# A hybrid decoder trunk on one core: the last two FFN pairs with tokens on partitions, attention scores in strict turn through one pipeline, two FFN pairs ahead, and activation parts side by side

## The chip, the cores and the metric

The kernel runs on one core of one Trainium2 chip. Times are device microseconds (us) of one execution; with one core, that core's time is the time of the kernel. Engines are named as in the profile: PE (TensorE), DVE (VectorE), ACT (ScalarE), POOL (GpSimd), SP (SyncE, here only an issuer of DMAs).

## The reference

`x` is (1, 512, 1024) float32, so 512 tokens of 1024 channels. The trunk has two layers and a final norm; D_FF is 2816.

```python
for l in range(2):
    if l == 0:
        h = h + conformer_conv(rmsnorm(h, norm_mix[0]), ...)   # pw1 + GLU, causal depthwise conv of 31, LayerNorm, silu, pw2
    else:
        if l == 1:
            k, v = split(rmsnorm(h, norm_kv) @ w_kv)           # 4 KV heads of 64
        q = (rmsnorm(h, norm_mix[1]) @ w_q)                    # 16 heads of 64
        h = h + banded_sink_attention(q, k, v, sinks, rel_bias) @ w_o
    gate, up = split(rmsnorm(h, norm_ffn[l]) @ w_up)
    h = h + (silu(gate) * up) @ w_down
return rmsnorm(h, norm_final)
```

The attention is banded: each block of 128 queries sees its own block of keys and the one before, with a relative-position bias, a window of 128 and one learned sink per head in the softmax.

## The kernel before, in words

**Layout.** Activations lie transposed: channels on partitions, the 512 tokens on the free axis. The residual `h` is one SBUF tile of [128, 8, 512] float32 that stays for the whole kernel; `x` comes in transposed and the result goes out transposed (`outT`).

**Products.** From the first FFN on, each fp32 product is made of three fp32r matmuls (`mm3`, L258 to L264): weights high part by activations high part, weights high by activations low, weights low by activations high, the first two at L262 and L263 and the third at L264, all into one PSUM bank (a bank holds 128 x 512 float32; there are eight). Weights are the stationary operand, activations (256 or 512 tokens wide) the moving one.

**Weights.** They stream from HBM in chunks of 512 KB in the order of `PLAN` (`chunk_plan`, L51 to L92). `get` (L244) hands out the next chunk, and `advance` (L191) issues the DMA six chunks ahead and the split three chunks ahead: ACT casts the high part (`whi`, L203), DVE subtracts to get the low part (`wlo`, L204). There are four buffers of each. The order of instructions on each engine is fixed by a scheduler when the kernel is built; `tc.issue_after` ties one instruction behind another.

**Layer 0.** Conv and the first part of the FFN (pairs 0 to 4 of 11; a pair is 256 hidden channels) are done for one half of the tokens (256) and then the other. While PE is at the first half's FFN, the depthwise conv of the second half runs beside it on POOL, ACT and DVE as background jobs (L207 to L226; taps L596 to L615), paced by due points. `ffn_part` (L423) calls `ffn_up` (L451), then two groups of down products; up takes four chunks for each pair: two halves of the 1024 input channels by gate and up. The normed input `xg` (`x0`) is an `Act` (L266): high tile and low tile apart. It is filled by `Next.on_h` (L511), which for each of the eight channel tiles has ACT scale (L382) and DVE subtract (L383), while `Rms` (L327) squares, adds (L340) and later makes the inverse root. `evac` (L455) takes a finished pair out of PSUM. The second part of FFN 0 (pairs 5 to 10) runs on all 512 tokens.

**Attention.** K and V, then q in two groups of eight heads (`down_group` with keys "q"), each ended by `q_evac` (L905). The heads are done in 16 units (`unit`, L912), each four heads of one group and one block of 128 queries: 12 score matmuls (L928) on 64 of the 128 rows, which go by turns to the two row halves (g = 0 and 1), four bias-and-minimum operations on DVE (L931), four exponentials on ACT (L938), a reciprocal (L940), four scalings on POOL (L942), transposes by PE (L950), cast and subtraction (L953, L954), the products with V by `mm3`, and cast and subtraction of the output (L968, L969). `pipeline(gp)` (L972) staggers the eight units of a group: one step starts a unit and advances three others. Pipeline `p0` (group 0) steps between the matmuls of q's second group, and what is left is drained behind it (L996); `p1` steps between the matmuls of the output projection's first half (o part 0) and is drained behind it (L1011).

**Layer 1's FFN and the end.** Pairs 0 to 5 and 6 to 8 run on all tokens. The last two pairs (`LAST`, 9 and 10) are followed by class `Fin` (L1020): two halves of 256 tokens, channels on partitions; each fetches the four down chunks, so they are fetched twice. `rows` adds to `h` (L1047), squares (L1051), and sums over channels by adds on POOL and matmuls with a column of ones (L1039); `sums` makes the mean (L1070), the inverse root by pow on POOL (L1072) and a diagonal (L1074); `spread` (L1084, L1088) brings the inverse root to all partitions by a matmul; `out_pool` (L1100) and `out_dve` (L1106) scale and store (L1096), two channel tiles by POOL and six by DVE.

## Time and profile before

| what | value |
|---|---|
| time of three runs | 1115.78, 1117.93, 1115.91 us (median 1115.91) |
| the profiled execution | 1115.77 us |
| its span in the profile | 1114.0 us, 15803 instructions |
| busy: PE, DVE, ACT, POOL | 1098.9, 662.3, 502.6, 322.1 us |
| mean granted TensorE clock | 0.993 of full speed |
| moved by DMA | 125.00 MB, 112 GB/s on average |

The span runs from the first to the last recorded instruction; the time of an execution holds a little more. A group line reads: line, engine, operation, out<-in, shapes, how often, then busy us and mean ns of one, then the idle time of that engine just before those instructions and what ended it. In a table of windows each engine has its busy us and instruction count, then the granted clock, the share of the DMA engines and GB/s. In a timeline, a row is start, duration, engine, line; a wait stands in brackets with what ended it. In the chain of waits each piece is the time that the last-ending chain spent there.

### The profile page before, as it was taken

To read this page: it belongs to the slowest core of one execution; us is meant where nothing else is said; L and a number is where in the kernel's file an instruction comes from. 1 tells how busy PE (TensorE), PEld (TensorE's weight loads), DVE (VectorE), ACT (ScalarE), POOL (GpSimd) and SP (SyncE) were. 2 spreads that over 40 slices of the span, in tenths; PEclk is the share of its full clock that TensorE was granted. 3 is DMA by queue.
4 is the path that set the end of the run, shared out by engine and by line. 5 is a ranking of instruction groups with operands and counts; after the bars stand their busy time and mean duration, and the time that the engine had idled before them with its cause. 6 is when DMAs were issued, how large, how long until landed. Compare 5 with 4: busy or idle time off the path is not lost.

```text
span 1114.0 us, 15803 instructions
## 1 busy us (share of the span) xinstructions
PE 1098.9 (99%) x5994; PEld 955.7 (86%) x5994; DVE 662.3 (59%) x1074; ACT 502.6 (45%) x891; POOL 322.1 (29%) x420
## 2 busy tenths in 40 slices
PE   9999998999999999999999999999999999999997
PEld 8888898999999888888888788888888888888886
DVE  4999999977665454443575686683444333444455
ACT  4786787765543232232343574553322211332233
POOL 4999699700100021110230332241111100110014
PEclk9999998999999999999999999999999999999998
DMA  9227044576655423332322201023233333323332
GB/s 362 100 31 84 25 168 136 183 247 190 189 174 184 135 95 101 105 97 95 95 95 87 75 29 48 30 95 95 95 95 95 97 102 103 96 95 95 95 95 77
DMA packets 40857, 125.00 MB, mean 112 GB/s; under 512 B 4395, under 2 KB 12748, under 8 KB 40780
## 3 DMA queue, kind: packets, MB, share of 16 engines
q1 hardware_dynamic: 40204, 123.55, 36.2%
q8 instruction: 47, 0.77, 0.3%
q10 hardware_dynamic: 576, 0.44, 0.1%
q14 instruction: 30, 0.25, 0.1%
HBM read 118.73 MB, written 5.24 MB: 111 GB/s over the span
## 4 chain that ended last, share of the span: by engine, by line
PE 90%; DVE 5%; ACT 2%; issue 1%; POOL 1%; DMA 0%; SPq 0%; POOLq 0%; DVEq 0%; ACTq 0%
PE bank L263 26%; PE bank L262 26%; PE bank L264 26%; PE bank L562 8%; PE bank L928 1%; DVE quad L383 1%; PE bank L649 1%; ACT pr L603 1%; DVE bank L611 1%; PE bank L950 1%; DVE wlo L204 1%; DMA h<-in_xT_dram 0%; DVE sc L931 0%; PE bank L375 0%; DVE ptl L954 0%
## 5 line engine op out<-in xcount | busy, mean ns | idle before, releaser
L263 PE MATMUL bank<-quad,whi 128*128 128x512 f32 (+1 forms) x1536 | 535.2, 349 | 3.8 <-DVE quad L383 3.7
L262 PE MATMUL bank<-quad,whi 128*128 128x512 f32 (+1 forms) x1536 | 534.8, 350 | 0.5 <-ACT quad L968 0.5
L264 PE MATMUL bank<-quad,wlo 128*128 128x512 f32 (+1 forms) x1536 | 535.1, 348 | 0.0
L204 DVE TENSOR_TENSOR wlo<-raw,whi 128x1024 fp32r<-128x1024 f32 x194 | 262.5, 1354 | 322.4 <-ACT whi L203 312.3
L203 ACT CAST whi<-raw 128x1024 fp32r<-128x1024 f32 x194 | 203.3, 1049 | 360.0 <-PE bank L263 319.3
L263 PEld LDWEIGHTS bank<-quad,whi 128*128 128x128 f32 x1536 | 292.0, 190 | 40.9 <-DVE quad L383 5.0
L262 PEld LDWEIGHTS bank<-quad,whi 128*128 128x128 f32 x1536 | 291.7, 190 | 38.5 <-ACT quad L968 0.9
L264 PEld LDWEIGHTS bank<-quad,wlo 128*128 128x128 f32 x1536 | 292.1, 190 | 36.8 <-issue 0.2
L472 POOL TENSOR_TENSOR tmp<-tmp,tmp 128x512 f32<-128x512 f32 x34 | 48.4, 1425 | 486.7 <-DVE tmp L471 473.1
L604 POOL TENSOR_TENSOR pr<-pr,pr 128x256 f32<-128x256 f32 x208 | 161.6, 825 | 11.0 <-ACT pr L603 11.0
L611 DVE SCALAR_TENSOR_TENSOR bank<-apad,wdw,bank 128x256 f32<-128x256 f32 x248 | 113.2, 485 | 3.6
L562 PE MATMUL bank<-quad,w 128*128 128x256 f32 x512 | 114.2, 382 | 0.6 <-DMA w<-in_W_dram 0.5
L562 PEld LDWEIGHTS bank<-quad,w 128*128 128x128 f32 x512 | 97.4, 191 | 15.4 <-DVE quad L537 1.7
L603 ACT ACTIVATE pr<-apad,wdw 128x256 f32<-128x256 f32 x208 | 99.0, 503 | 20.8 <-POOL pr L604 18.1
L340 POOL TENSOR_TENSOR tmp<-tmp,tmp 128x256 f32<-128x256 f32 (+1 forms) x35 | 38.8, 1109 | 138.6 <-ACT tmp L336 109.1
L470 ACT ACTIVATE tmp<-tmp 128x512 f32<-128x512 f32 x34 | 21.4, 632 | 92.9 <-DVE tmp L469 92.9
L942 POOL TENSOR_SCALAR sc<-sc,sm 128x256 f32<-128x256 f32 (+1 forms) x64 | 30.0, 489 | 79.4 <-DVE sm L940 79.4
L386 ACT CAST quad<-tmp 128x512 fp32r<-128x512 f32 (+1 forms) x50 | 29.1, 586 | 30.4 <-POOL tmp L472 26.6
L471 DVE TENSOR_TENSOR tmp<-bank,rsbc 128x512 f32<-128x512 f32 x34 | 23.5, 691 | 32.4 <-PE bank L264 32.4
L383 DVE SCALAR_TENSOR_TENSOR quad<-h,prm,quad 128x512 fp32r<-128x512 f32 (+1 forms) x40 | 39.5, 1020 | 0.5 <-ACT quad L382 0.4
L938 ACT ACTIVATE sc<-sc,m 128x257 f32<-128x257 f32 (+1 forms) x64 | 30.3, 476 | 15.4 <-DVE m L931 13.7
L387 DVE TENSOR_TENSOR quad<-tmp,quad 128x512 fp32r<-128x512 f32 (+1 forms) x50 | 32.8, 661 | 2.5 <-ACT quad L386 2.5
(140 smaller groups left out, 747.0 us busy)
## 6 DMA issues: line engine op xcount, KB each, us to landing
raw<-in_W_dram SPq DMA_DIRECT2D x202, 512.0 KB, 3.5
w<-in_W_dram SPq DMA_DIRECT2D x15, 512.0 KB, 9.7
fd<-fs SPq DMA_DIRECT2D x1, 3072.0 KB, 33.8
h<-in_xT_dram SPq DMA_DIRECT2D x8, 256.0 KB, 5.9
bias<-fd SPq DMA_DIRECT2D x8, 256.0 KB, 5.5
out_dram<-res SPq DMA_DIRECT2D x14, 128.0 KB, 1.8
w<-in_W_dram SPq DMA_DIRECT2D x2, 256.0 KB, 4.1
out_dram<-res ACTq DMA_DIRECT2D x2, 128.0 KB, 2.7
```

Of the source, the lines that this page charges most:

```text
L203: nc.scalar.copy(hi, r)
L204: lo_engine[0].tensor_sub(lo, r, f32(hi))
L262: nc.tensor.matmul(out, w[0], x[0], start=start, stop=False)
L263: nc.tensor.matmul(out, w[0], x[1], start=False, stop=False)
L264: nc.tensor.matmul(out, w[1], x[0], start=False, stop=stop)
L340: self.eng.tensor_add(sq, self.acc, sq)
L383: nc.vector.scalar_tensor_tensor(dst[1], src, g, f32(dst[0]), op0=ALU.mult, op1=ALU.subtract)
L472: nc.gpsimd.tensor_mul(t2, t1, t2)
L562: mm = nc.tensor.matmul(self.pb[:, w * W2:(w + 1) * W2], w1[ct][:, w, k, :], x[k] if x else xg[k][:, tok], start=k == 0, stop=k == KT - 1)
L603: on_act = nc.scalar.mul(pr, a[:, j:j + W2], tap(j))
L604: on_pool = nc.gpsimd.tensor_add(pr, acc, pr)
L611: on_dve = nc.vector.scalar_tensor_tensor(yt if i == nd - 1 else c, src, tap(i), c if i else self.shift, op0=ALU.mult, op1=ALU.add)
```

## The change

- **Two pairs ahead.** `up_order(lo, hi, ahead)` gives the order of the up chunks. In the FFN of the first token half the second half of pair 0 and the first half of pair 1 change places: (0,0), (1,0), (0,1), (1,1), then as before. `PLAN` follows. Both pairs' `evac` stand behind (1,1).
- **Parts side by side.** `x0` becomes `Pairs`: high and low part of a channel tile lie next to each other in one tile ([128, 2, 2, 512]). In the FFN of the second token half (`twin=True`) a product is two matmuls (`mm2`): the weights' high part by both parts at once, 512 wide, into the two halves of a bank, and the weights' low part by the high part, 256 wide, into the first half. Each output tile then takes a whole bank (four a pair); the two halves are added when they are taken out (ACT copy, DVE add), and POOL does the multiplication that DVE did.
- **Attention.** Each unit starts with a 1x1 matmul, and its 12 score matmuls are tied behind each other and behind it by `issue_after`. There is one pipeline over 16 units. It steps between the matmuls of q's second group, whose `q_evac` is done bank by bank as each finishes; four more steps follow; then it steps in o part 0 and is drained behind that.
- **The end.** `Block` takes the place of `Fin`: four blocks of 128 tokens, tokens on partitions. The residual comes into PSUM by eight transposes of `h` tiles into two banks, and the down products of the last two pairs are added to it there with the activations as stationary operand and the weights as moving one (512 wide, three matmuls per 128 channels and half of D). ACT squares a bank with a running sum, DVE and POOL make the inverse root, DVE multiplies by the final gain (fetched once as a row to all partitions), ACT and DVE scale by the inverse root, and the result goes out as (512, 1024). The first two blocks share each fetched down chunk, and the other two use the same splits, so the four chunks are fetched once.

```diff
@@ -48,6 +48,13 @@
 NPARAM = _c
 
 
+def up_order(lo, hi, ahead):
+    o = [(pair, half) for pair in range(lo, hi) for half in range(2)]
+    if ahead:
+        o[1], o[2] = o[2], o[1]
+    return o
+
+
...
+    class Pairs:
+
+        def __init__(self, n, w=512):
+            self.per = 1024 // w
+            self.q = [quads.tile([P, self.per, 2, w], F32R, tag="quad", name=uid("quad")) for _ in range(-(-n // self.per))]
+
+        def both(self, i):
+            return self.q[i // self.per][:, i % self.per]
+
+        def __getitem__(self, i):
+            b = self.both(i)
+            return b[:, 0, :], b[:, 1, :]
+
+    def mm2(out, w, x, start, stop):
+
+        first, second = (w[0], x, out), (w[1], x[:, 0, :], out[:, 0, :])
+        if stop:
+            first, second = second, first
+        nc.tensor.matmul(first[2], first[0], first[1], start=start, stop=False)
+        nc.tensor.matmul(second[2], second[0], second[1], start=False, stop=stop)
 
...
-            if on_step is not None and ci == nk - 1:
+                if on_m is not None and ci == nk - 1 and k == 1:
+                    on_m(m)
+                    if m % 2:
+                        on_step()
+            if on_step is not None and on_m is None and ci == nk - 1:
                 on_step()
                 on_step()
...
+            if twin:
+                banks = [bank().rearrange("p (a s) -> p a s", a=2) for _ in range(4)]
+                for kp in range(lo, hi):
+                    whi, wlo = get("down", layer, kp, g)
+                    order = [(k, m) for k in range(2) for m in range(4)]
+                    if kp == hi - 1:
+                        order = [(k, m) for m in range(4) for k in range(2)]
+                    for k, m in order:
+                        sl = slice(m * P, (m + 1) * P)
+                        mm2(banks[m], (whi[:, k, sl], wlo[:, k, sl]), hid.both(2 * (kp - lo) + k),
+                            kp == lo and k == 0, kp == hi - 1 and k == 1)
+                rs_bc = rms.step2()
+                for m, b in enumerate(banks):
+                    t, hm = temp()[:, 0:w], h[g * 4 + m][:, tok]
+                    nc.scalar.copy(t, b[:, 1, :])
+                    nc.vector.tensor_add(t, b[:, 0, :], t)
+                    nc.gpsimd.tensor_mul(t, t, rs_bc)
+                    nc.vector.tensor_add(hm, hm, t)
+                continue
...
+            if twin:
+                t1, t2 = temp(), temp()
+                for which, t in enumerate((t1, t2)):
+                    for m in range(2):
+                        b = banks[which * 2 + m]
+                        tm = t[:, m * w:(m + 1) * w]
+                        nc.scalar.copy(tm, b[:, 1, :])
+                        nc.vector.tensor_add(tm, b[:, 0, :], tm)
+                t1v, t2v = (t.rearrange("p (a s) -> p a s", a=2) for t in (t1, t2))
+                nc.gpsimd.tensor_mul(t1v, t1v, rs_bc.unsqueeze(1).to_broadcast([P, 2, w]))
+                nc.scalar.activation(t1, t1, AF.Silu)
+                nc.gpsimd.tensor_mul(t2, t1, t2)
+                i = 2 * (pair - lo)
+                q = hid.q[i // 4][:, i % 4:i % 4 + 2]
+                nc.scalar.copy(q[:, :, 0, :], t2v)
+                nc.vector.tensor_sub(q[:, :, 1, :], t2v, f32(q[:, :, 0, :]))
+                return
...
+        opened, pending = {}, []
+        for pair, half in up_order(lo, hi, ahead):
+            if half == 0:
+                if twin:
+                    opened[pair] = [bank().rearrange("p (a s) -> p a s", a=2) for _ in range(4)]
+                    opened[pair] = opened[pair], opened[pair]
+                elif w == 256:
+                    full = [bank(), bank()]
+                    opened[pair] = full, [b[:, e * w:(e + 1) * w] for b in full for e in range(2)]
+                else:
+                    full = accs(w)
+                    opened[pair] = full, full
+            full, banks = opened[pair]
+            for which in range(2):
+                whi, wlo = get("up", layer, pair, half, which)
+                order = [(k, m) for k in range(4) for m in range(2)]
+                if half == 1:
+                    order = [(k, m) for m in range(2) for k in range(4)]
+                for k, m in order:
+                    sl = slice(m * P, (m + 1) * P)
+                    if twin:
+                        mm2(banks[which * 2 + m], (whi[:, k, sl], wlo[:, k, sl]), xg.both(half * 4 + k)[:, :, tok],
+                            half == 0 and k == 0, half == 1 and k == 3)
+                        continue
+                    mm3(banks[which * 2 + m], (whi[:, k, sl], wlo[:, k, sl]), cut(xg[half * 4 + k], tok),
+                        half == 0 and k == 0 and opens(m, w), half == 1 and k == 3 and closes(m, w))
+            if half == 0 and w == 512 or half == 0 and twin:
                 rms.step1()
+            if half == 1 and w == 256 and pair == lo and not twin:
+                rms.step1()
+            if half == 1:
                 pending.append((pair, full))
-            else:
-                evac(pair, full)
+            if half == (1 if ahead else 0) or w == 512 or twin or pair > lo:
+                if not (half == 1 and pair == lo and w == 256 and not twin):
+                    for p in pending:
+                        evac(*p)
+                    pending = []
         return hid
...
-        x0 = {"ffn0": Act(KT)}
+        x0 = {"ffn0": Pairs(KT)}
...
+    ffn_part(0, 0, x0["ffn0"], HALF[1], n1.rms, twin=True)
...
+        def q_evac(g, banks, ms=range(4)):
+            if qs[g] is None:
+                qs[g] = (quad(), quad())
+            for m in ms:
                 t = temp()
                 nc.vector.scalar_tensor_tensor(t, banks[m], -HD ** -0.5, rs_bc, op0=ALU.mult, op1=ALU.mult)
                 split((qs[g][0][:, m, :], qs[g][1][:, m, :]), t)
...
+
+            mm = nc.tensor.matmul(pbs[1][0:1, 0, 0:1], ones_c, ones_c, start=True, stop=True)
             for e in range(2):
                 j = 2 * jp + e
                 for a, b in ((0, 0), (0, 1), (1, 0)):
                     for g in range(2):
-                        nc.tensor.matmul(pbs[g][:, e, :], qs[gp][a][rows[g], j, qt],
-                                         kq[rows[g], b, gp, k0:k0 + BAND], start=a + b == 0, stop=a == 1)
+                        with tc.issue_after(mm.ins):
+                            mm = nc.tensor.matmul(pbs[g][:, e, :], qs[gp][a][rows[g], j, qt],
+                                                  kq[rows[g], b, gp, k0:k0 + BAND], start=a + b == 0, stop=a == 1)
...
-        def pipeline(gp):
-            units = [unit(gp, jp, n) for n in range(NBLK) for jp in range(2)]
-            done = 0
+        def pipeline():
+            units = [unit(gp, jp, n) for gp in range(2) for n in range(NBLK) for jp in range(2)]
             for t in range(len(units) + 4):
                 for d in (4, 3, 1, 0):
...
-        p0 = pipeline(0)
+        pipe = pipeline()
+
+        def step():
+            next(pipe, None)
+
         banks = [bank() for _ in range(4)]
         down_group([(("q", kp, 1), 2 * kp) for kp in range(4)], lambda kt: xq[kt], banks,
-                   on_step=lambda: next(p0, None))
-        q_evac(1, banks)
-        drain(p0)
-        p1 = pipeline(1)
+                   on_step=step, on_m=lambda m: q_evac(1, banks, [m]))
+        for _ in range(4):
+            step()
         nxt = Next(("ffn1",))
...
+                drain(pipe)
...
+
+    res = ctx.enter_context(tc.tile_pool(name="res", bufs=2))
+    gain = res.tile([P, D], F32, tag="gain", name="gain", bufs=1)
+    nc.sync.dma_start(gain, fin.to_broadcast([P, D]))
     hid = ffn_up(1, *LAST, nxt.x["ffn1"], ALL, nxt.rms)
...
+    chunks = {}
+
+    class Block:
+        def __init__(self, b):
+            self.b, self.tok = b, slice(b * P, (b + 1) * P)
+            self.banks = [bank(), bank()]
+            self.ss = small.tile([P, 4], F32, tag="ss", name=uid("ss"))
+            self.hg = []
+            for i in range(KT):
+                c = (i % 4) * P
+                nc.tensor.matmul(self.banks[i // 4][:, c:c + P], h[i][:, self.tok], ident, is_transpose=True,
+                                 start=i % 4 == 0, stop=False)
 
         def down(self, kp, g):
+            if (kp, g) not in chunks:
+                chunks[kp, g] = get("down", 1, kp, g)
+            whi, wlo = chunks[kp, g]
+            for k in range(2):
+                a = cut(hid[2 * (kp - LAST[0]) + k], self.tok)
+                for n, (x, w) in enumerate(((a[0], whi), (a[0], wlo), (a[1], whi))):
+                    nc.tensor.matmul(self.banks[g], x, w[:, k, :], start=False, stop=kp == LAST[1] - 1 and k == 1 and n == 2)
+
+        def half(self, g):
+            ss, b = self.ss, self.banks[g]
+            sq = res.tile([P, 512], F32, tag="sq", name=uid("sq"))
+            nc.scalar.activation(sq, b, AF.Square, accum_out=ss[:, g:g + 1])
+            if g == 0:
+                nc.vector.tensor_scalar(ss[:, 2:3], ss[:, 0:1], 1.0 / D, EPS, op0=ALU.mult, op1=ALU.add)
+            else:
+                nc.vector.scalar_tensor_tensor(ss[:, 3:4], ss[:, 1:2], 1.0 / D, ss[:, 2:3], op0=ALU.mult, op1=ALU.add)
+                rs = small.tile([P, 1], F32, tag="rs1", name=uid("rs1"))
+                nc.gpsimd.tensor_tensor(rs, ss[:, 3:4], mhalf[:, 0:1], op=ALU.pow)
+                self.rs = rs
+            t = res.tile([P, 512], F32, tag="hg", name=uid("hg"), bufs=5)
+            nc.vector.tensor_mul(t, b, gain[:, g * 512:(g + 1) * 512])
+            self.hg.append(t)
+
+        def out(self, w):
+            for c in range(0, 512, w):
+                for g, t in enumerate(self.hg):
+                    t = t[:, c:c + w]
+                    if g:
+                        nc.vector.tensor_scalar(t, t, self.rs[:, 0:1], None, op0=ALU.mult)
+                    else:
+                        nc.scalar.mul(t, t, self.rs[:, 0:1])
+                    (nc.sync if g else nc.scalar).dma_start(out[self.tok, g * 512 + c:g * 512 + c + w], t)
+
+    pairs = range(*LAST)
+    first = [Block(0), Block(1)]
+    for kp in pairs:
+        for g in range(2):
+            for bl in first:
+                bl.down(kp, g)
+                if kp == LAST[1] - 1:
+                    bl.half(g)
+    for bl in first:
+        bl.out(512)
+    for b in range(2, NBLK):
+        bl = Block(b)
+        for g in range(2):
+            for kp in pairs:
+                bl.down(kp, g)
+            bl.half(g)
+        bl.out(512 if b < NBLK - 1 else 256)
```

All of `Fin`, with `fill` and what calls it, is removed; `kernel` passes the final gain as a row and takes the output as (512, 1024).

179 lines of the change are left out of this document (20 added, 159 removed).

## The prediction

> **What bounds the kernel now.** I read the busy shares first, then the chain of work that ended last by engine, the waits of TensorE (PE), and the table of windows.
>
> ```profile
> PE 1098.9 (99%) x5994; PEld 955.7 (86%) x5994; DVE 662.3 (59%) x1074; ACT 502.6 (45%) x891; POOL 322.1 (29%) x420
> ...
> PE 90%; DVE 5%; ACT 2%; issue 1%; POOL 1%; DMA 0%; SPq 0%; POOLq 0%; DVEq 0%; ACTq 0%
> ```
> ```profile
> PE bank L263 <- DVE quad L383: 3.7, 3, 1.9
> ```
> ```profile
> core 0: us, PE busy (x) PEld busy (x) DVE busy (x) ACT busy (x) POOL busy (x), PEclk, DMA share, GB/s
> ...
> 167.00:177.30 10.30, 7.33 (x34) 6.63 (x33) 10.20 (x11) 7.92 (x17) 10.30 (x11) 0.67 0.28 95
> ...
> 250.00:300.00 50.00, 50.00 (x419) 50.00 (x419) 36.37 (x47) 26.38 (x41) 6.48 (x8) 1.00 0.62 187
> ...
> 640.00:660.00 20.00, 19.66 (x140) 17.18 (x139) 19.05 (x55) 16.40 (x49) 9.09 (x20) 1.00 0.14 49
> 760.00:1000.00 240.00, 240.00 (x1059) 198.38 (x1058) 99.09 (x103) 67.92 (x79) 22.76 (x17) 1.00 0.31 97
> ```
>
> PE is the bound, at a full granted clock, almost everywhere: 90% of the chain. So time comes from two sources only: fewer or cheaper matmuls, or one of the few places where PE stands. The largest wait that the trace names is 3.7 us, behind DVE's L383, in the stretch at 167 us; there the clock also falls to 0.67. Two spacings come out of the windows and price all that follows: 50/419 = **0.1193 us** for a 256-wide matmul, 240/1059 = **0.2266 us** for a 512-wide one (a busy time of one matmul is longer, since they are pipelined). A 512-wide matmul is 0.012 cheaper than two of 256. DVE and ACT hold 59% and 45%, so their work is free except where a window shows them full: 167 to 177 and the middle of attention, 640 to 660.
>
> The profiled execution took 1115.77 us, its span 1114.0, so 1.77 lie outside the span. The sum is made against 1115.77, which is 0.14 below the median 1115.91; that difference is nothing here. About 0.2% (2.2 us) is what a measurement of this kernel can tell from no change.
>
> **A: two pairs ahead (first-half FFN of layer 0).** Up's third chunk needs the upper four tiles of xg, which DVE is late with:
>
> ```profile
> 161.06 0.47 PE L262 MATMUL bank<-quad,whi 128*128 128x256 f32 x1
> ...
> 168.16 0.94 DVE L383 SCALAR_TENSOR_TENSOR quad<-h,prm,quad 128x256 fp32r<-128x256 f32 x1
> 169.16 0.39 PE L263 MATMUL bank<-quad,whi 128*128 128x256 f32 x1 [1.88 <-DVE quad L383]
> 170.90 0.58 PE L263 MATMUL bank<-quad,whi 128*128 128x256 f32 x1 [0.99 <-DVE quad L383]
> ...
> 175.13 3.42 DVE L204 TENSOR_TENSOR wlo<-raw,whi 128x1024 fp32r<-128x1024 f32 x2
> ...
> 177.31 0.31 PE L264 MATMUL bank<-quad,wlo 128*128 128x256 f32 x1
> ...
> 179.62 0.36 PE L262 MATMUL bank<-quad,whi 128*128 128x256 f32 x1
> ```
>
> The new order puts pair 1's two first-half chunks ahead of that wait. Four chunks of 24 matmuls run from 161.06 to 161.06 + 96×0.1193 = 172.5 with nothing late. Then the fifth needs xg's upper tiles and its own wlo. That wlo is still made on DVE behind the same eight L383/sum operations: the L204 pair that starts at 175.13 gives it at about 175.13 + 1.71, or 177.3 with one more conv tap ahead of it. So **the wait doesn't vanish, it turns into one of 4.8 us for wlo** (172.5 to 177.3). The fifth chunk starts 2.3 us earlier than the 179.62 of now. Against that: PE's clock fell after waits of 1.88 and 0.99, and after a wait of 4.8 the clock would fall as well, and a third of it missing (0.67) over some 4.5 us costs 1.5; and the next chunks' wlo come one by one from a DVE and a POOL that are full (10.20 and 10.30 of 10.3 us), so the lead is likely eaten there. Bounds: +2.3 saved if the lead is kept, 2 lost if the cold clock and the supply both count. I take **0**.
>
> **B: x's parts side by side (second-half FFN of layer 0).** In that FFN 480 up and 240 down matmuls of 256 become 240 of 512 (whi by [xhi|xlo]) and 240 of 256 (wlo by xhi). Per triple: 3×0.1193 = 0.3579 becomes 0.2266 + 0.1193 = 0.3459, so 240×0.012 = **+2.9**. The added adds and copies (estimates from the rows of like width under C: ACT about 6.9, DVE 7.8, POOL 2.9 us a pair) fit under a pair's 32×0.3459 = 11.07 us of PE, and a pair now holds four banks until then, with eight in all. Bounds 0 (the saved share is lost in bank waits) to 2.9; I take the row's value, since both widths are measured in long undisturbed windows. The Trainium skill, "TensorE: Matmul & The Clock Gate", section "Back-to-back issue gap", gives an isolated gap of N/2.4 + 2.5 ns, so 109 and 216 ns; it also says that this over-counts a sustained stream at large N. By that formula B would be an estimated 0.6. The trace's spacings speak against it (119.3 and 226.6 ns).
>
> **C: attention.** Scores first:
>
> ```profile
> 616.18 0.97 PE L928 MATMUL bank<-kq,quad 64*128 64x256 f32 x12
> 617.08 0.50 PE L262 MATMUL bank<-quad,whi 128*128 128x512 f32 x1
> ...
> 628.29 0.97 PE L928 MATMUL bank<-kq,quad 64*128 64x256 f32 x6
> 629.19 0.49 PE L262 MATMUL bank<-quad,whi 128*128 128x512 f32 x1
> ...
> 646.13 0.40 PE L264 MATMUL bank<-quad,wlo 128*128 128x512 f32 x1
> ...
> 664.13 0.73 PE L262 MATMUL bank<-quad,whi 128*128 128x512 f32 x2 [0.19 <-ACT quad L968]
> ```
> ```profile
> 646.65 0.87 PE bank L950 x8
> ...
> 653.83 0.91 PE bank L928 x6
> 654.73 0.32 PE bank L262
> ```
> ```profile
> L1007 DVE TENSOR_TENSOR h<-bank,h x16: 662/685/693, 676.9 to 741.7; 128x512 f32<-128x512 f32 x16
> ```
>
> Twelve scores whose row halves alternate take 0.90 us (616.18 to 617.08); where the scheduler issued them as 6 and 6, each six take 0.90 as well (628.29 to 629.19). Four units are split so, which strict turn repairs: 4×0.9 = 3.6 less, and 1.2 for the extra groups' ends (the product behind a group stands with 0.32 instead of 0.12 in the chain of waits, 653.83 to 654.73), 4.8 in all. The drains add 2.3 us of short PE waits. The price is one 1x1 dummy per unit, 16 of 0 to 0.2.
>
> What decides is the stretch without o's or q's products. Now it runs from 646.13 to 664.13, 18 us. After, o's first product needs the same last unit of group 0, but the one pipeline has moved four units of group 1 ahead into the stretch, in place of p0's drain. DVE's rows:
>
> ```profile
> L931 DVE CUSTOM_DVE_ANT_0 sc<-bank,bias,sk 128x256 f32<-128x256 f32 x48 | 20.6, 477 | 0.6 <-PE bank L928 0.5
> L931 DVE CUSTOM_DVE_ANT_0 sc<-bank,bias,sk 128x128 f32<-128x128 f32 x16 | 4.7, 349 | 2.3 <-PE bank L928 2.3
> L931 DVE DVE_READ_ACCUMULATOR2_ANT m<- 128x1 f32 x64 | 5.2, 82 | 0.0
> L954 DVE TENSOR_TENSOR ptl<-bank,pth 128x512 fp32r<-128x512 f32 x28 | 19.1, 687 | 4.4 <-ACT pth L953 4.0
> L969 DVE TENSOR_TENSOR quad<-bank,quad 128x256 fp32r<-128x256 f32 x16 | 6.7, 418 | 11.4 <-ACT quad L968 11.3
> L940 DVE RECIPROCAL sm<-sm 128x4 f32<-128x4 f32 x16 | 2.8, 174 | 5.6 <-ACT sc L938 5.6
> ```
> ```profile
> L204 DVE TENSOR_TENSOR wlo<-raw,whi 128x1024 fp32r<-128x1024 f32 x194 | 262.5, 1354 | 322.4 <-ACT whi L203 312.3
> ```
> ```profile
> L938 ACT ACTIVATE sc<-sc,m 128x257 f32<-128x257 f32 x48 | 24.0, 503 | 7.3 <-DVE m L931 5.6 <-POOL sc L921 1.6
> L938 ACT ACTIVATION_READ_ACCUMULATOR sc<-sc,m 128x1 f32 x64 | 12.0, 188 | 0.0
> L953 ACT CAST pth<-bank 128x512 fp32r<-128x512 f32 x28 | 16.2, 587 | 4.9 <-PE bank L264 2.7 <-DVE ptl L954 1.5 <-PE bank L950 0.7
> ```
>
> Six units' bias steps (four of 4×(477+82) = 2.24, two of the first block, 1.72) are 12.4; eleven L954 7.6; six L969 2.5; five L940 0.9; the last bank of q (three operations of 512, by L954's 687) 2.1; one L204 1.35: **26.9 us of DVE**. PE has 44 transposes at 0.87/8 = 0.109 (4.8), 61 products at 0.1193 (7.3) and six score groups at 0.90 + 0.2 (6.6): 18.7. ACT has 4×(503+188) + 2×587 and about 0.4 for the output's cast, 4.3 a unit. So DVE bounds the stretch and o starts near 646.1 + 0.4 + 26.9 = 673.4, 9.3 later than now, but with four units fewer left. From there PE has 192×0.2266 = 43.5 for o, four score groups (4.4), 52 transposes (5.7), 95 products (11.3) and the dummies (0.4): 65.3, to 738.7. Now o's last product ends with part 1's last add (near 741.5 by the L1007 row). So **+2.8**. Bounds: if DVE's work before 646 has been further along, so that PE sets the stretch at 18.7 plus small gaps, +10; if each unit's chain shows half of ACT's conversions beside DVE, 6 to 7 us more, -4. DVE was 19.05 of 20 us busy in 640 to 660 while ACT was 16.40: they overlap well, and DVE is the engine without slack. That is why I take its sum.
>
> **D: the last two pairs with tokens on partitions.**
>
> ```profile
> 1101.05 0.28 PE L264 MATMUL bank<-quad,wlo 128*128 128x256 f32 x1
> ...
> 1109.29 1.04 ACTq L1096 DMA_DIRECT2D out_dram<-res  x2
> ```
> ```profile
> L1070 DVE TENSOR_SCALAR ms<-bank 128x2 f32<-128x2 f32 x2 | 0.3, 160 | 1.2 <-PE bank L1039 1.2
> ```
> ```profile
> L1072 POOL TENSOR_TENSOR rs<-ms,mhalf 128x2 f32<-128x2 f32 x2 | 1.4, 710 | 2.7 <-DVE ms L1070 2.7
> ```
>
> PE now issues 192 down matmuls of 256 (191 spacings, 22.8) and four small sums (about 0.36): 23.15 until the last one starts at 1101.05. Then 12.95 pass to the span's end at 1114.0: sums, pow, diagonal, spreading, scaling, and the DMAs. After: 32 transposes (3.5) and 96 of 512 (95 spacings, 21.5): 25.0, so **1.85 more of PE**. The tail after the last matmul starts: the matmul 0.39, a Square of 512 (587 + 188), the mean on DVE (160), pow on POOL (710), two scalings of 256 (503 by the L938 row of that width), two DMA issues (1.04 by the ACTq row), then what follows now from the issues' end, 1114.0 - 1110.33 = 3.67, and some 0.2 of handing over: 0.39+0.78+0.16+0.71+1.0+1.04+3.67+0.2 = **7.9**, against 12.95. Balance 5.05 - 1.85 = **+3.1**. Pair 10's hidden tile isn't ready when up ends; 16 transposes and 24 products of pair 9, 7.2 us, lie over its five steps of 0.7 and one on POOL of some 1.4 (an estimate from the rows of like width), about 5. The chunks are fetched once instead of twice, which frees DMA, ACT and DVE that aren't late here. Bounds +2 (the order of two scalings and issues behind pow costs one more) to +5 (scalings side by side on two engines; a faster landing).
>
> **Sum.** 0 + 2.9 + 2.8 + 3.1 = 8.8 less: 1115.77 - 8.8 = **1107.0**.
>
> **Rivals.**
> 1. *DVE doesn't bind attention.* For it: PE's 18.7 against ACT and DVE that have room before 640. Against: the 640 to 660 window. C = 10, total 16: 1099.8. Chance 0.17.
> 2. *The saved matmuls save nothing* (B = 0, C and D as far as they are matmuls, the rest stays): 2.9 less and 1.2 of C: 1111. Against it are the spacings. Chance 0.10. The Trainium skill's formula, above, leads near this case.
> 3. *Slower: in the stretch after q, ACT and DVE take turns.* With one unit's chain waiting for the next (scores, DVE, exp, transposes, cast, subtraction), each of the six units takes DVE's 4.5 and half of ACT's 4.3 and more. It decides from 6.0 us a unit (8.8/6 = 1.5 above the 4.5 eats all gains); at 6.7, which is half of ACT's time in the open, the stretch is 13 longer: 1120. Against: the same two engines overlap in 640 to 660. Chance 0.10.
> 4. *"Ahead" does as it says* and the 7.3 us of stretch 167 to 177 go wholly: 1115.77 - 16 = about 1100. It needs wlo earlier than the rows allow. Chance 0.05.
>
> **How the numbers follow.** The forecast has 0.58. Its own range, from the bounds of A (-2 to 2.3), B, C and D of which not all fall together, is 1102 to 1112. To hold 8 in 10 the range takes in rivals 1, 2 and 4 on the fast side and stops at **1113** above and **1099** below, since rival 3 and the far end of C (-4 with A at -2) are the 2 in 10 left out. Faster by over 0.2%: the forecast but for its worst corner (0.55), rivals 1, 4 and 2 (0.17 + 0.05 + 0.10, less 0.03): 0.84. Slower: 0.09. Within: 0.07.
>
> **What would show it.** A: a wait of some 5 us near 172 for L204, where L383's stood; none there would make A's term wrong. B: 3 us less from the start to the end of the second half's FFN, with no bank wait. C: DVE full for about 27 us after q's last product, o's first product near 27 us after it, and no score group of six. D: up's last to the last matmul about 25 us, then 8 to the end. A stretch after q of 36 us or more would make the sign wrong.

## The result, and the profile after

The changed kernel takes 1109.77 us (median of five, 1109.03 to 1110.12) against 1115.99 before (1115.78 to 1117.93): a ratio of 0.9944, 95% interval 0.9933 to 0.9956. That is 6.2 us less; the forecast was 8.8 less. The profiled execution took 1109.03 us with a span of 1107.0, so 2.0 us lie outside the span.

From the page of after, busy times and the chain that ended last by engine:

```profile
PE 1090.6 (99%) x5696; PEld 933.4 (84%) x5696; DVE 662.5 (60%) x1077; ACT 507.3 (46%) x914; POOL 329.3 (30%) x425
...
PE 87%; issue 5%; ACT 3%; DVE 3%; POOL 1%; DMA 0%; SPq 0%; POOLq 0%
```

PE still bounds, with 298 instructions and 8.3 us of busy time less. To see where the 7.0 us of span went, I cut both traces at the same matmuls. These are rows of PE's timeline, before and then after: the first product of the second half's FFN, of layer 0's second FFN part, of q, of the second pair of layer 1's FFN, and the last up product; ahead of them, for after, the first product of the first half's FFN (161.06 before, shown with the forecast).

```profile
283.19 0.28 PE L262 MATMUL bank<-quad,whi 128*128 128x256 f32 x1
...
370.44 0.40 PE L262 MATMUL bank<-quad,whi 128*128 128x512 f32 x1
...
591.58 0.40 PE L262 MATMUL bank<-quad,whi 128*128 128x512 f32 x1
...
761.76 0.79 PE L262 MATMUL bank<-quad,whi 128*128 128x512 f32 x1
...
1077.47 0.39 PE L264 MATMUL bank<-quad,wlo 128*128 128x512 f32 x1
```
```profile
161.40 0.47 PE L267 MATMUL bank<-quad,whi 128*128 128x256 f32 x1
...
286.26 0.40 PE L299 MATMUL bank<-quad,whi 128*128 128x512 f32 x1
...
371.61 0.39 PE L267 MATMUL bank<-quad,whi 128*128 128x512 f32 x1
...
592.73 0.40 PE L267 MATMUL bank<-quad,whi 128*128 128x512 f32 x1
...
759.86 0.79 PE L267 MATMUL bank<-quad,whi 128*128 128x512 f32 x1
...
1075.57 0.39 PE L269 MATMUL bank<-quad,wlo 128*128 128x512 f32 x1
```

| stage | before | after | gain | forecast |
|---|---|---|---|---|
| A: first half's FFN, second half's output projection (from 161.06 / 161.40) | 122.13 | 124.86 | -2.7 | 0 |
| B: second half's FFN | 87.25 | 85.35 | +1.9 | +2.9 |
| FFN part two and K/V | 221.14 | 221.12 | 0 | 0 |
| C: q, attention, o, and pair 0 of layer 1's up (23.2 in both) | 170.18 | 167.13 | +3.05 | +2.8 |
| the rest of layer 1's FFN, up to the last up product | 315.71 | 315.71 | 0 | 0 |
| D: from there to the end of the span | 36.53 | 31.43 | +5.1 | +3.1 |

With 0.34 that after starts later this is the 7.0 of the spans. The table carries the study: the stages repeat in every profile of a kernel that has the same part, A with the lead lies between 124.77 and 124.87 in eight profiles, without it between 121.92 and 122.13 in six; B without parts side by side at 87.25 or 87.26 in four. What varies from run to run is the start of the FFN (160.97 to 162.82), although the order of instructions up to there is the same with and without the lead; so a difference under 1 us between medians is read from the stages. PE's waits in after (total, times, longest):

```profile
PE bank L269 <- DVE wlo L209: 4.6, 2, 3.3
PE bank L267 <- ACT rsbc L395: 1.5, 1, 1.5
PE bank L267 <- ACT pth L1032: 1.2, 3, 0.5
...
PE bank L401 <- ACT tmp L388: 0.6, 1, 0.6
```

Stage A's waits for L383 (1.88 and 0.99) are gone; 6.7 us of waits for low parts, the spread root and the scaled identity (4.6 + 1.5 + 0.6) have come in the same stage.

### The profile page after: what moved, and what is told of

It reads as the page before. It is cut to its first block, busy times and chain, and to the rows that moved or that the text cites. A ratio compares the mean times of both kernels' runs of the same rounds, so it can differ in the third digit from the quotient of the medians.

```text
span 1107.0 us, 15216 instructions
## 1 busy us (share of the span) xinstructions
PE 1090.6 (99%) x5696; PEld 933.4 (84%) x5696; DVE 662.5 (60%) x1077; ACT 507.3 (46%) x914; POOL 329.3 (30%) x425
## 4 chain that ended last, share of the span: by engine, by line
PE 87%; issue 5%; ACT 3%; DVE 3%; POOL 1%; DMA 0%; SPq 0%; POOLq 0%
PE bank L268 22%; PE bank L267 22%; PE bank L269 22%; PE bank L637 8%; PE bank L299 5%; PE bank L300 3%; PE bank L1124 1%; PE bank L1007 1%; POOL pr L679 1%; PE bank L1029 1%; ACT pr L678 1%; PE bank L724 1%; DVE quad L409 1%; DVE bank L686 0%; DVE wlo L209 0%
## 5 line engine op out<-in xcount | busy, mean ns | idle before, releaser
L269 PE MATMUL bank<-quad,wlo 128*128 128x512 f32 (+1 forms) x1232 | 449.0, 365 | 4.6 <-DVE wlo L209 4.6
L267 PE MATMUL bank<-quad,whi 128*128 128x512 f32 (+1 forms) x1232 | 448.5, 365 | 1.5 <-ACT rsbc L395 1.5
L268 PE MATMUL bank<-quad,whi 128*128 128x512 f32 (+1 forms) x1232 | 448.4, 364 | 0.9 <-DVE quad L409 0.9
L208 ACT CAST whi<-raw 128x1024 fp32r<-128x1024 f32 x190 | 199.3, 1049 | 332.6 <-PE bank L268 282.2
L269 PEld LDWEIGHTS bank<-quad,wlo 128*128 128x128 f32 x1232 | 233.2, 189 | 41.0 <-DVE wlo L209 5.0
L267 PEld LDWEIGHTS bank<-quad,whi 128*128 128x128 f32 x1232 | 233.3, 189 | 38.6 <-ACT rsbc L395 1.7
L268 PEld LDWEIGHTS bank<-quad,whi 128*128 128x128 f32 x1232 | 233.2, 189 | 37.4 <-DVE quad L409 1.3
L679 POOL TENSOR_TENSOR pr<-pr,pr 128x256 f32<-128x256 f32 x208 | 158.3, 810 | 10.9 <-ACT pr L678 10.9
L299 PE MATMUL bank<-quad,whi 128*128 128x512 f32 x212 | 75.9, 398 | 0.0
L300 PE MATMUL bank<-quad,wlo 128*128 128x256 f32 x212 | 59.3, 280 | 0.0
L299 PEld LDWEIGHTS bank<-quad,whi 128*128 128x128 f32 x212 | 39.7, 188 | 8.4
```

What stands on the lines that cost most here:

```text
L208: nc.scalar.copy(hi, r)
L267: nc.tensor.matmul(out, w[0], x[0], start=start, stop=False)
L268: nc.tensor.matmul(out, w[0], x[1], start=False, stop=False)
L269: nc.tensor.matmul(out, w[1], x[0], start=False, stop=stop)
L299: nc.tensor.matmul(first[2], first[0], first[1], start=start, stop=False)
L300: nc.tensor.matmul(second[2], second[0], second[1], start=False, stop=stop)
```

## The experiments

Times are medians against the kernel before, measured beside them; "ratio" is against it.

**1. The lead off** (`no_ahead`).

```diff
-        ffn(0, *HALVES0[0], ahead=hf == 0)
+        ffn(0, *HALVES0[0])
...
-        ffn_part(0, 0, x0["ffn0"], HALF[0], n0.rms, ahead=True)
+        ffn_part(0, 0, x0["ffn0"], HALF[0], n0.rms)
```

> The changed kernel with the up chunks of the first half's FFN in the old order; all else as changed. Theory (the lead of two pairs only turns the wait for L383 into later and longer waits, 3.28 for wlo, 1.48 for the spread inverse root, 1.28 for wlo again): the stretch from the first up product to the end of the second half's conv sums is 2.7 us shorter, 1107.0 us. Rival (those waits come from the later finish of x's tiles and have nothing to do with the order; the lead is neutral, as forecast): 1109.8 us.

1106.04 us (ratio 0.9907, 0.9893 to 0.9921): 3.7 less than the changed kernel. Stage A falls to 121.97, 2.9 less, and no other stage changes. The lead costs; the other 0.8 is within the variation of the start.

**2. Parts side by side off** (`no_twin`), and the same without the lead (`noahead_notwin`): the diff takes `twin=True` away and makes `x0` an `Act` again.

> The changed kernel with the second half's FFN as before (three matmuls of 256, high and low parts in tiles apart). Theory (512-wide matmuls that stand between 256-wide ones cost 0.2345 instead of 0.2266, so a triple saves 0.006 to 0.008 and not 0.012): 1.9 us slower than the changed kernel, 1111.7 us. Rival (the forecast's price holds and the rest of it is lost at the edges): 2.9 slower, 1112.7 us. Rival (nothing is saved): 1109.8 us.

> The changed kernel without the two pairs ahead and without parts side by side. The run with the lead off took 1106.0 us. Theory (the stage of the second half's FFN is 2.1 us longer without parts side by side, and nothing hides that): 1108.2 us. Rival (the small difference of the run with only that part off, 0.4 to 0.7 us, is what it is worth): 1106.6 us.

1110.47 us (0.9947, 0.9935 to 0.9958) and 1108.50 us (0.9935, 0.9921 to 0.9948): 0.7 more than with it beside the lead, 2.5 more without the lead. In both, stage B is 87.26 against 85.35, so 1.9; the two times stand on either side of it. The stage went as the theory had it, and the one median of 0.7 alone would have misled.

**3. No 1x1 matmul** (`no_dummy`).

```diff
-            mm = nc.tensor.matmul(pbs[1][0:1, 0, 0:1], ones_c, ones_c, start=True, stop=True)
+            mm = None
...
-                        with tc.issue_after(mm.ins):
+                        with tc.issue_after(mm.ins) if mm is not None else nullcontext():
```

> The changed kernel without the 1x1 matmul that opens each attention unit; its 12 scores stay tied behind each other. Theory (16 dummies take 0.12 us of PE each and hide nothing): 1.9 us faster than the changed kernel, 1107.9 us. Rival (the dummy takes up a wait or keeps the order, so that without it the gain goes into waits of the scores for their banks): 1109.8 us or slower.

1108.11 us (0.9923, 0.9911 to 0.9935), 1.7 less; by the stage, attention is 0.9 less. Theory and rival are both half right. The dummies' 1.92 us go, but the scores take 16.95 us in place of 14.86 (what a kind of matmul takes is added up from each one's start to the next matmul's start). PE's timeline of this kernel shows why: one score leaves the group, and the other eleven follow later.

```profile
629.60 0.38 PE L1007 MATMUL bank<-kq,quad 64*128 64x256 f32 x1
629.91 0.50 PE L267 MATMUL bank<-quad,whi 128*128 128x512 f32 x1
...
631.49 0.97 PE L1007 MATMUL bank<-kq,quad 64*128 64x256 f32 x11
```

The single one holds PE 0.31 us (629.60 to 629.91). The eleven take their 0.90 all the same. Eight of 16 groups are broken so. By the code the dummy writes into the second bank, so it can take the single score's place in a wait for that bank; in the changed kernel the twelve stay together, for 0.12 us a dummy. That this is how it keeps them together is argued from the order alone. What is left of the gain is 1.05 us less at transposes and value products.

**4. The new end alone** (`block_only`: the changed kernel with the lead, parts side by side, ties, dummies and one pipeline all put back as before).

> The kernel before with the new end alone: tokens on partitions for the last two pairs, everything else (order of up, x's parts, pipelines, scores) as before. Theory (the end is worth what its stage shows, 1.7 more of PE and 6.8 less behind the last matmul): 5.1 us faster than before, 1110.9 us. Rival (a part of the gain needs the shift of what stands ahead): as forecast 3.1, 1112.9 us.

1111.37 us (0.9953, 0.9941 to 0.9965), 4.9 less than before (1116.26 beside it). Stage D is 31.5 us, as in the changed kernel: it needs nothing of the other parts.

**5. The changed kernel again, on one chip with the two runs that follow** (`after_again`).

> The changed kernel itself, beside the three others on one chip. Both theories: 1109.8 us, and a stretch of the first half's FFN with the same four PE waits (3.3, 0.6, 1.5 and 1.3 us) if they come from a fixed order, other sizes if they hang on the timing of POOL and of the DMAs.

1109.78 us (0.9945, 0.9933 to 0.9958). Stage A is 124.8 again with waits of 3.92, 0.59 and 1.32: sizes move between the waits and the stage does not. That is the first sign that the end of the stage is set elsewhere.

**6. No ties, no dummies, one pipeline** (`no_chain`), **and ties with two pipelines** (`two_pipes`). The first drops `issue_after` and the 1x1; the second puts `pipeline(gp)`, `p0`, `p1`, both drains and the late `q_evac` back.

> The changed kernel with neither ties between the scores nor the 1x1 matmul, one pipeline kept. In the built order 60 of the 192 scores then stand behind one of their own row half, in groups of 4 and 8, and there are 22 groups for 16. Theory (a score behind one of its own half costs 0.15 instead of 0.075 us, a group's ends 0.2): 60 x 0.075 + 6 x 0.2 = 5.7 more, 1.9 less for the dummies, so 3.8 slower than the changed kernel: 1113.6 us. Rival (the turn doesn't matter, DVE sets the stretch): 1109.8 us or 1.9 less.

> The changed kernel with two pipelines, each drained, and q taken out after the group, as before; scores tied and dummies kept. Theory (one pipeline only saves PE the short waits in the drains, 26.3 us of value products before and 24.6 after): 1.7 slower than the changed kernel, 1111.5 us. Rival (with the scores tied, the drains have no stalls left, or DVE's work moved into the stretch after q costs what the waits give): 1109.8 us or less.

1111.21 us (0.9957, 0.9945 to 0.9970) and 1111.69 us (0.9963, 0.9950 to 0.9975): 1.4 and 1.9 more than the changed kernel. Attention takes 170.18 us before, 169.07 with one pipeline alone, 169.48 with ties alone, 167.13 with both: 1.1 and 0.7 apart, 3.05 together. For `no_chain` the scores themselves are as dear as the theory had it, 20.57 us against 14.86 and 1.92 of dummies, 3.8 more; PE's timeline has them in sixes,

```profile
649.81 0.97 PE L1006 MATMUL bank<-kq,quad 64*128 64x256 f32 x6
...
651.50 0.97 PE L1006 MATMUL bank<-kq,quad 64*128 64x256 f32 x6
```

but PE's time at transposes, products and value products falls by 1.9 meanwhile, so that half of what the untied scores cost comes back there. With ties and two pipelines the reverse is seen; the cheaper scores (14.80) are partly waited away again in the drains, value products taking 27.12 us in place of 26.28 before and 24.63 after. This is PE's wait for the subtraction of low parts in that kernel, 1.4 us where after has 0.3:

```profile
PE bank L268 <- DVE ptl L1033: 1.4, 2, 1.0
```

**7. The sums of squares behind the fifth low part** (`late_sums`), to test what the lead waits for.

```diff
-            self.rms.add(h[i][:, self.tok])
+            if self.late is not None and i >= 4:
+                self.late.append(i)
+            else:
+                self.rms.add(h[i][:, self.tok])
+
+        def add_late(self):
+            for i in self.late:
+                with tc.issue_after(split_ins[12]):
+                    self.rms.add(h[i][:, self.tok])
...
+            if half == 0 and w == 256 and not twin and pair == lo + 1:
+                n0.add_late()
```

> The changed kernel with the lead of two pairs kept, but the last four sums of squares of the first token half tied behind the fifth chunk's low part on DVE (before, four sums of 0.96 us each stand among the last four L409, all ahead of that low part). Theory (the lead's first wait is for a low part that stands behind those sums): the low part is ready about 3.5 us sooner, the wait of 3.3 to 3.9 us falls to under 1, and the stage of the first half's FFN with the second half's output projection falls from 124.8 to 122 to 123: about 1107.5 us. Rival (the inverse root comes later by as much, so that the waits for it and for later low parts grow): stage 124.8 or more, 1109.8 us.

1108.98 us (0.9937, 0.9925 to 0.9950), and stage A is 124.87 us, unchanged to 0.01. The edit does its part: the fifth chunk's low part is ready at 172.97 us in place of 176.71, and the wait of 3.28 for it is gone. But PE then waits 0.76 for the sixth low part, 1.19 for the eighth and 2.60 for the scaled identity of the inverse root, so the theory falls and the rival holds. PE's waits in this kernel:

```profile
PE bank L270 <- DVE wlo L210: 3.2, 3, 1.3
PE bank L402 <- ACT tmp L389: 2.6, 1, 2.6
```

**8. Low parts of the probabilities made once** (`no_ptl`).

```diff
-                nc.vector.tensor_sub(lo, pt, f32(hi))
-                pts.append((hi, lo))
+                if first_lo[0] is None:
+                    first_lo[0] = at.tile([P, 512], F32R, tag="lo1", name="lo1", bufs=1)
+                    nc.vector.tensor_sub(first_lo[0], pt, f32(hi))
+                pts.append((hi, first_lo[0]))
```

> The changed kernel with the low part of the transposed probabilities made once, for the first block, and used for all others: 27 subtractions of 0.69 us less on DVE, PE's work the same. It leaves those low parts out of the computation. The stretch between q's last and o's first product is 21.4 us in the changed kernel, with DVE busy 19.8 of it. Forecast's theory (DVE sets that stretch): it falls to some 18.7 us, PE's own sum, and attention by at least 2.7: 1107 us or less. Rival (PE sets it, with short waits for both engines): only the wait for the low part goes, 0.3 to 1 us: 1109.3 us.

1106.79 us (0.9915, 0.9901 to 0.9928), 3.0 less; attention is 2.5 shorter. The stretch between q's last and o's first product, here in the table of windows for after and for this kernel:

```profile
core 0: us, PE busy (x) PEld busy (x) DVE busy (x) ACT busy (x) POOL busy (x), PEclk, DMA share, GB/s
...
647.25:668.63 21.38, 20.90 (x192) 17.86 (x190) 19.77 (x72) 18.68 (x64) 9.43 (x26) 1.00 0.09 27
```
```profile
651.28:669.90 18.62, 18.62 (x170) 16.13 (x168) 12.21 (x53) 16.41 (x57) 9.41 (x25) 1.00 0.09 31
```

With DVE relieved PE is full in that stretch, and the profile lists no wait of PE in attention any more. But 21.38 and 18.62 don't hold the same work: the edit changes the built order too, seven units instead of six have their scores ahead of q's last product, and the stretch has 170 of PE's matmuls for 192. The 2.5 us of all attention, where the work is the same, can be compared; they lie between the rival's 1 and the theory's 2.7. So the subtractions cost PE time; the run can't tell their sum, their place in each unit's chain and the new order apart.

**9. Without lead and dummies** (`noahead_nodummy`), **and with the sums late as well** (`noahead_late_nodummy`, the four sums tied behind the last L409).

> The changed kernel without the lead of two pairs and without the 1x1 matmuls. The parts measured apart: lead off 3.7 less by time and 2.8 by its stage, 1x1 off 1.7 less by time and 1.0 by its stage. Theory (they are apart in time and add up): stages give 3.8 less, 1106.0 us; times give 5.4 less, 1104.4 us.

> The kernel of the run before this one, and the last four sums of squares of the first token half tied behind the last L409 on DVE. Theory (the two waits of 1.9 and 1.0 us for L409, and the seven microseconds at half clock behind them, come from sums that stand among the L409): the second wait goes, the clock falls later or not at all, 1 to 4 us less than the run without this edit. Rival (the first wait of 1.9 is enough to bring the clock down, and the sums come late for the inverse root): within 1 us of it.

1105.70 us (0.9905, 0.9890 to 0.9920) and 1105.49 us (0.9901, 0.9888 to 0.9915). Both beat the changed kernel, by 4.1 and 4.3; from each other they can't be told. The stages add up (121.92 for A as with the lead off, attention as without the dummies); the times' sum of 5.4 was too much. The late sums take the wait of 1.0 for L409 down to 0.5 in two pieces, and win nothing: the wait of 1.91 remains, and the clock falls to 0.50 behind it, as these windows show.

```profile
171.00:173.00 2.00, 1.74 (x10) 1.32 (x11) 2.00 (x3) 1.85 (x4) 2.00 (x3) 0.94 0.43 174
173.00:175.00 2.00, 2.00 (x11) 2.00 (x11) 1.93 (x3) 1.42 (x3) 2.00 (x4) 0.50 0.00 0
```

## Why the prediction was right, point by point

The total was right by its range and its sign, with 2.6 us too much gain. Three of four terms were mis-sized, by -2.7, -1.0 and +2.0 us, and the fourth is right by three errors; that they cancel as far as they do is luck.

**A was taken as 0 and is -2.7 by its stage.** The step up to the first wait went as written: the lead's wait for L383 turned into one for wlo (3.28 us where 4.8 was worked out). What failed is the step after it, "the lead is likely eaten there", with 2 lost as its bound: it is eaten, and 2.7 more. Where this happens can be seen at the low part of the fourteenth up chunk. These are DVE's row that makes it and PE's first product with it, before, then with the lead off, then after:

```profile
206.09 1.26 DVE L204 TENSOR_TENSOR wlo<-raw,whi 128x1024 fp32r<-128x1024 f32 x1
...
207.98 0.28 PE L264 MATMUL bank<-quad,wlo 128*128 128x256 f32 x1
```
```profile
206.66 1.25 DVE L209 TENSOR_TENSOR wlo<-raw,whi 128x1024 fp32r<-128x1024 f32 x1
...
207.97 0.39 PE L269 MATMUL bank<-quad,wlo 128*128 128x256 f32 x1
```
```profile
209.09 1.81 DVE L209 TENSOR_TENSOR wlo<-raw,whi 128x1024 fp32r<-128x1024 f32 x1
...
210.96 0.39 PE L269 MATMUL bank<-quad,wlo 128*128 128x256 f32 x1 [1.28 <-DVE wlo L209]
```

Before, this low part is ready 0.6 us ahead of its use (207.35 and 207.98); with the lead off it is used as soon as it is ready (207.91 and 207.97). So in the old order too the stage hangs on it, or nearly: with this low part where it stands, no more than 0.6 us was to be won ahead of it, and not 2.3. The six profiles without the lead bear this out. PE's waits in their stage A add up to between 2.8 and 4.3 us, the granted clock is at 0.50 from 171 to 177 us before and at 1.00 throughout in `block_only`, and the stage takes 121.9 to 122.1 in all of them. With the lead PE takes this low part 49.5 us after the start of the FFN in all eight profiles, in place of 46.4 with the lead off, and what follows takes 75.3 us in place of 75.5.

Why it comes 3.1 us later is read from traces and not tried. In after, the chain that ended last runs back from it over ACT's queue to POOL's conv taps. From 167.0 to 202.6 us every piece of that chain is POOL's own ("issue" is POOL's time between them, in which it waits for nothing that the profile shows); with the lead off the chain runs from 176 us on along PE.

```profile
by line: issue 78.8%; POOL pr L679 15.9%; POOL y L690 5.1%; POOL rs L380 0.3%
```

The forecast also left out the inverse root that evacuation waits for. In the new order its sums come behind the sixth chunk in place of the fourth, and its pow moves back in POOL's queue, which is full of conv taps until 211.5 us. Timeline rows of POOL, ACT and DVE with the lead off, then after, then POOL's alone with the late sums:

```profile
185.80 0.70 POOL L380 TENSOR_TENSOR rs<-ms,mhalf 128x2 f32<-128x2 f32 x1
...
192.90 0.35 ACT L395 COPY rsbc<-bank 128x256 f32<-128x256 f32 x1
...
193.79 1.28 DVE L527 TENSOR_TENSOR tmp<-bank,rsbc 128x512 f32<-128x512 f32 x2
```
```profile
190.95 0.70 POOL L380 TENSOR_TENSOR rs<-ms,mhalf 128x2 f32<-128x2 f32 x1
...
199.29 0.35 ACT L395 COPY rsbc<-bank 128x256 f32<-128x256 f32 x1
...
200.17 1.28 DVE L527 TENSOR_TENSOR tmp<-bank,rsbc 128x512 f32<-128x512 f32 x2
```
```profile
190.78 0.70 POOL L381 TENSOR_TENSOR rs<-ms,mhalf 128x2 f32<-128x2 f32 x1
```

The pow stands 5.1 us later with the lead (190.95 against 185.80), the spread root 6.4, and the first evacuation 6.4. It stands at the same place when the first wait is taken away (190.78). From 199 us on, two pairs are evacuated at once on DVE and ACT, among the casts and subtractions that make the low parts. That the first wait does not matter is shown by the late sums. The pow itself is 0.3% of the chain, so its own place need not be what counts; POOL's full queue and the bunched evacuation are what is left, and which of them adds the 3.1 us stays open. The rival that the whole 7.3 us would go is out; its 7.3 was PE's busy time in the window 167 to 177.3, where 34 matmuls at 0.1193 are 4.1 us, so that PE lost some 6.2 there.

**B was 2.9 and is 1.9.** The mechanism is right; the size of a 512-wide matmul between 256-wide ones is off. In the window 300 to 370 of after,

```profile
300.00:370.00 70.00, 70.00 (x400) 60.88 (x399) 49.80 (x55) 38.13 (x56) 18.24 (x14) 1.00 0.56 188
```

400 matmuls, half of each width, take 0.350 a pair, where 0.3459 was put together from pure streams; PE waits for nothing there, as forecast. Up and down products show it alike (0.234 to 0.236 for the wide one, 0.117 for the narrow one), so the layout of x isn't the reason; which it is stays open. The Trainium skill's formula ("TensorE: Matmul & The Clock Gate", "Back-to-back issue gap"), estimated at 0.6 in the forecast, lies 1.3 below the stage, the row's price 1.0 above it.

**C was 2.8 and is 3.05, by luck: three errors cancel, and the step on DVE failed.** The forecast let DVE's sum set the stretch after q, 27.3 us with its 0.4 ahead. The stretch is 21.38, and PE is busy for 20.90 of it, DVE for 19.77. The chain that ended last runs there for 78% along PE's own matmuls and for 2% along DVE's ptl:

```profile
by line: PE bank L1007 21.2%; PE bank L1029 19.1%; PE bank L267 13.3%; PE bank L268 12.4%; PE bank L269 8.8%; ACT sc L1017 7.0%; issue 5.3%; ACT pth L1032 4.7%; PE bank L1001 2.8%; DVE ptl L1033 2.2%; POOL sc L1021 1.8%; ACT quad L1047 1.2%
```

So it is nearer to the forecast's 18.7 for PE's own work, which had left out 0.7 for the dummies and 0.2 for q's last product; some 1.7 us are short waits and switches (an estimate, the difference of these numbers). DVE's sum was too long. These are its groups in that window:

```profile
L1033 DVE TENSOR_TENSOR ptl<-bank,pth 128x512 fp32r<-128x512 f32 x11 | 7.5, 687 | 0.5 <-ACT pth L1032 0.2
L1010 DVE CUSTOM_DVE_ANT_0 sc<-bank,bias,sk 128x256 f32<-128x256 f32 x16 | 6.7, 476 | 0.0
L1010 DVE CUSTOM_DVE_ANT_0 sc<-bank,bias,sk 128x128 f32<-128x128 f32 x8 | 2.4, 344 | 0.0
L1048 DVE TENSOR_TENSOR quad<-bank,quad 128x256 fp32r<-128x256 f32 x5 | 2.1, 417 | 1.1 <-ACT quad L1047 1.1
L1010 DVE DVE_READ_ACCUMULATOR2_ANT m<- 128x1 f32 x24 | 2.0, 82 | 0.0
L209 DVE TENSOR_TENSOR wlo<-raw,whi 128x1024 fp32r<-128x1024 f32 x1 | 1.2, 1208 | 0.0
L1019 DVE RECIPROCAL sm<-sm 128x4 f32<-128x4 f32 x5 | 0.8, 170 | 0.0
L413 DVE TENSOR_TENSOR quad<-tmp,quad 128x512 fp32r<-128x512 f32 x1 | 0.7, 685 | 0.0
L985 DVE SCALAR_TENSOR_TENSOR tmp<-bank,rsbc 128x512 f32<-128x512 f32 x1 | 0.7, 680 | 0.0
```

The instructions were counted nearly right: one L1048 and one of q's three operations fewer. But counts times means add up to 25.4 us while the window has DVE busy for 19.77: the records of neighbours overlap, so a sum of durations is 28% too long.

The other two errors go the other way. Behind the stretch the forecast's 65.3 us were 2.8 too short (668.63 to 736.68): o's products, broken up by others, take 0.236 on average and not 0.2266, and value products 13.2 us and not 11.3. And the end that it compared with was 2.9 too late: 741.5 was near the last add of o on DVE, while PE in the kernel before had started layer 1's up at 738.58:

```profile
738.58 0.39 PE L262 MATMUL bank<-quad,whi 128*128 128x512 f32 x1
```

With the measured stretch of 21.38 its own sum would have given 8.7 us.

By kinds of work, attention's 3.05 are 4.06 from the scores (4.8 forecast), 1.65 from value products and their waits (2.3 forecast), less 1.92 for dummies (1.6 or less) and 0.75 more for products and transposes. The condition of the first rival (DVE doesn't bind) is nearer to the trace than the forecast's step, but its 10 us did not come, since it shares the other two errors. The third (engines in turn) is out: the stretch is 3.6 a unit.

**D was 3.1 and is 5.1.** PE's part was 25.0 and is 25.31 (1075.57 to the last product at 1100.88); the tail was 7.9 and is 6.12. Rows of POOL, ACT and ACT's DMA queue at the end of after:

```profile
1102.27 0.55 POOL L1135 TENSOR_TENSOR rs<-ss,mhalf 128x1 f32<-128x1 f32 x1 [5.79 <-DVE ss L1133]
1102.85 0.91 ACT L1148 ACTIVATE hg<-hg,rs 128x256 f32<-128x256 f32 x2 [0.85 <-POOL rs L1135]
...
1103.38 0.83 ACTq L1149 DMA_DIRECT2D out_dram<-hg  x2
```

Pow on one column takes 0.55 (0.71 forecast); the first store is issued while the second half is scaled, so that scaling and issuing take 1.36 us (1102.85 to 1104.21) where 2.04 was put one behind the other; and from the issues' end to the span's end it is 2.79 where 3.67 was taken over. The rest is in the old end, 36.53 us from the last up product where 23.15 + 12.95 = 36.10 had been put together.

The slower rival did not come; the lead by itself is slower, by more than the bound of 2 that the forecast gave it, and no rival had named that.

## What to carry to other kernels

A wait that ends last on the bound engine is worth removing only if what it releases is not pinned again further on: follow what the stage needs next, here a low part that is used some 37 us after that wait, before a lead is credited. Price an operation in the mix that it will stand in, and an engine's work by its busy time in a window and not by a sum of durations. Undo each part alone and read its stage: two parts that win 1.1 and 0.7 us apart won 3.05 together, and one part of a change that won 6.2 lost 2.8.

## What the runs showed of the hardware that was not expected

- A 512-wide fp32r matmul takes 0.234 to 0.236 us between 256-wide ones (after, second half's FFN) and 0.2266 in a stream of its own (before, 760 to 1000 us); a wide and a narrow one add to 0.350.
- A single 64-row score that leaves its group costs 0.31 us, and the eleven that follow take the 0.90 us of all twelve (`no_dummy`).
- After waits of 1.91 and two of 0.25 us within four microseconds (`noahead_late_nodummy`) the granted clock fell to 0.50, as it had after 1.88 and 0.99 before. After 1.33, 1.00 and 0.77 within six (`block_only`) it stayed at 1.00.
